# A late row is stored only where its token has its last late expert; GpSimd gathers the last eight tiles, then the last expert's sums

## The chip, the core and the metric

One core of one Trainium2 chip runs the kernel. The time is device microseconds of one launch. TensorE (PE) multiplies matrices, VectorE (DVE) and ScalarE (ACT) work on elements, GpSimd (POOL) does a few element operations and issues every transfer whose rows are found by an index, SyncE (SP) issues plain transfers; 16 DMA engines move the data.

## What is computed

One layer of a hybrid block over 2048 tokens of width 1024 in float32: a mixer (gated short convolution beside a gated delta rule), then a mixture of 32 experts in which each token goes to two, then a root-mean-square norm. What the change touches is the end:

```python
x = x + concat([y_a, y_b]) @ w_out              # after the mixer
h = rms_norm(x, ffn_norm_g)
# two experts e for every token, with a gate each:
y_e = (silu(h @ w_gate[e]) * (h @ w_up[e])) @ w_down[e]
x = x + sum(gate_e * y_e for the token's two experts)
return rms_norm(x, final_norm_g)
```

## The kernel before

The first 1150 us compute the mixer; the tokens' sums `x` then lie in DRAM as `acc_d`, the normed rows as `h2_d` (`h_d` in the profile), the gates as `gt_d`. While that ends, the router finds each token's experts (`OH`, `pos`) and, for every expert, a table of its tokens: `tabG` (rows to gather), `tabS` (rows to scatter to; an empty place has an index beyond the last row and is skipped) and `gix`. The experts are ranked by their number of tokens, and each rank has a fixed capacity of rows (`CAPS`); the last three ranks (`LAST = 3`, the "late" experts) have 120, 116 and 112 rows.

The loop over `jobs` runs the 32 experts. For each, SP loads the weights through staging tiles (`mst`) and ACT and DVE split them into float16 pairs (`wgu`, `wd`, L92 and L93); GpSimd gathers the expert's rows (`xr`, L1014) and gates (`gs`, L1019); PE turns them and multiplies (`gate_up`, L1045; `down`, L1080 or L1115); ACT scales the result into `yo`, and GpSimd adds it to the tokens' rows of `acc_d` by a scatter that accumulates (L1058). A scheduler orders each engine's instructions by the order of the code, woven by `weave`, and by `issue_after`, which puts an instruction behind another.

The final norm runs beside the last experts. The 2048 tokens are 16 tiles of 128. A token without a late expert is finished before the last three experts are, so its row can be normed early: `bix` holds a tile's row numbers, and for a token with a late expert an index beyond the last row. `load` (L1342) gathers a tile's rows of `acc_d` by `bix`: tiles 0 to 7 early into `mst`, tiles 8 to 15 late into `xw`. `norm_all` squares four tiles on ACT (`square`, L1330), makes one over the root on DVE and GpSimd (`root`, L1333 and the power at L1334), multiplies by it and by the gain on DVE (`gain`, L1337), and stores: tiles below `NPL` with a plain store by SP (L1374), the others by GpSimd with `bix` (L1378), so that rows of late tokens are left out.

The late tokens come last. `rows_of` (L1385) gathers for the last expert (rank 31, 112 rows) its tokens' rows of `acc_d` into `J.base`, here called the base; this can start only when the scatter of rank 30 has landed. DVE adds the last expert's result to it (L1087), and it is written back to `acc_d` without accumulating (L1406). The same gather fetches into `ends` the rows of ranks 29 and 30 (120 and 116 rows). All three are normed (`norm_rows`) and stored by `tabS` (`store_rows`, L1396). A token may have two late experts; then its row stands in two of the three sets, and only the later set has the whole sum. So these three stores write the same rows of `out` and are held in order: each waits until the one before has landed.

Around the change the order on GpSimd is: scatter of rank 30, base, two `ends`, eight late tiles (`load_late` puts them behind the last of the `rows_of`), the write of the base, the powers, four stores by `bix`, three by `tabS`. A GpSimd transfer uses one of eight semaphores in turn and waits until the transfer eight before it has landed.

## Time and profile before

| | us |
|---|---|
| median of 3 runs | 1951.93 (1949.07 to 1955.11) |
| the profiled execution | 1950.76 |
| its span | 1949.0 |
| PE busy | 1750.1 (90%) |
| DVE busy | 1402.3 (72%) |
| ACT busy | 1007.7 (52%) |
| POOL busy | 426.6 (22%) |

The span is the time from the first to the last instruction on the chip; the profiled execution took 1.76 us more around it. Busy shares are means over stages with different limits: the last PE instruction ends at 1880.3 us, so the last 69 us have no matrix work, and what lies there is read from the waits and the order of time in that stretch. The times in the sections below are microseconds from the start of the span.

### The profile page before, as it was taken

The numbers are of one execution on the slowest core, as the hardware profiler recorded it, in microseconds if no ns is written. First come the engines' busy times: TensorE is split into PE (matmuls) and PEld (weight loads), VectorE is DVE, ScalarE is ACT, GpSimd is POOL, SyncE is SP. The second block draws the span as 40 slices with busy tenths as digits, with TensorE's granted clock in tenths as the row PEclk, the third lists the DMA queues.
The fourth block names the chain that finished last, engine by engine and source line by source line (L and its number), as shares of the span: only waits on it lengthen the run. The fifth ranks groups of instructions, "written<-read, shape, count | busy, mean of one in ns | idle before, by whom it ended". The sixth has DMA issues, their size and how long they took to land.

```text
span 1949.0 us, 41805 instructions
## 1 busy us (share of the span) xinstructions
PE 1750.1 (90%) x16213; PEld 1198.9 (62%) x16213; DVE 1402.3 (72%) x2708; ACT 1007.7 (52%) x1674; POOL 426.6 (22%) x375
## 2 busy tenths in 40 slices
PE   7789999999999999999999959999989999999840
PEld 5455555555555554444454438788888899999730
DVE  8989888888888745322244768887778888888732
ACT  5655434444444324211234636766667777777621
POOL 1321111121111100000000012233222344344343
PEclk9989999999999999999999979999999999999975
DMA  4122001001001105002255967999999999999873
GB/s 143 67 64 56 11 15 44 18 11 47 20 11 37 36 19 165 28 15 57 98 175 197 342 231 236 347 306 311 309 315 349 360 332 345 349 343 316 286 233 136
DMA packets 203597, 330.27 MB, mean 169 GB/s; under 512 B 44590, under 2 KB 98935, under 8 KB 203394
## 3 DMA queue, kind: packets, MB, share of 16 engines
q1 hardware_dynamic: 178738, 271.20, 40.8%
q0 software_dynamic: 20128, 47.30, 9.5%
q10 hardware_dynamic: 4528, 9.06, 1.2%
q8 instruction: 129, 2.11, 0.4%
q14 instruction: 74, 0.61, 0.1%
HBM read 276.05 MB, written 54.82 MB: 170 GB/s over the span
## 4 chain that ended last, share of the span: by engine, by line
PE 31%; DMA 17%; DVE 9%; issue 5%; ACT 3%; SPq 1%; POOL 1%; DVEq 0%; ACTq 0%; POOLq 0%
PE acc L134 11%; PE a L1045 9%; DMA mst<-in_w_up_dram 9%; PE a L965 5%; DMA mst<-in_w_down_dram 4%; DVE wgu L93 2%; DMA mst<-in_w_gate_dram 2%; ACT wgu L92 1%; SPq L766 1%; PE pn L548 1%; DMA end<-acc_d,tabG 1%; PE pl L1102 1%; DVE yt L1121 1%; DVE xT L1031 1%; DVE wd L93 1%
## 5 line engine op out<-in xcount | busy, mean ns | idle before, releaser
L134 PE MATMUL acc<-hT,whl 128*128 128x512 f16 x2640 | 635.4, 381 | 0.2 <-DVE hT L203 0.2
L134 PEld LDWEIGHTS <-whl 128*128 128x128 f16 x2640 | 252.8, 99 | 248.4 <-issue 11.3
L1045 PE MATMUL a<-xT,wgu 128*128 128x128 f16 (+17 forms) x6144 | 394.8, 227 | 5.0 <-DVE sl L1052 2.2
L1045 PEld LDWEIGHTS <-wgu 128*128 128x128 f16 x6144 | 388.7, 99 | 12.0 <-issue 6.3
L93 DVE SCALAR_TENSOR_TENSOR wgu<-mst,gw,wgu 128x1024 f16<-128x1024 f32 x256 | 317.6, 1276 | 20.1 <-ACT wgu L92 19.6
L92 ACT ACTIVATE wgu<-mst,gw 128x1024 f16<-128x1024 f32 x256 | 280.2, 1139 | 34.8 <-DMA mst<-in_w_up_dram 32.7
L965 PE MATMUL a<-wo,yb 128*128 128x512 f16 x768 | 176.0, 381 | 0.0
L93 DVE SCALAR_TENSOR_TENSOR wd<-mst,wd 128x1024 f16<-128x1024 f32 x128 | 154.1, 1214 | 4.1 <-ACT wd L92 4.1
L1058 POOL DMA_INDIRECT acc_d<-yo,tabS x50 | 96.8, 1936 | 262.2 <-ACT yo L1106 190.2
L92 ACT ACTIVATE wd<-mst 128x1024 f16<-128x1024 f32 x128 | 131.2, 1047 | 21.4 <-DMA mst<-in_w_down_dram 21.4
L1115 PE MATMUL a<-ac,wd 128*128 128x144 f16 (+12 forms) x1824 | 136.3, 230 | 2.8 <-ACT ac L92 1.7
L1115 PEld LDWEIGHTS <-wd 128*128 128x128 f16 x1824 | 124.2, 98 | 5.4 <-issue 3.8
L965 PEld LDWEIGHTS <-yb 128*128 128x128 f16 x768 | 72.1, 98 | 79.4 <-issue 2.7
L294 DVE SCALAR_TENSOR_TENSOR cv<-raw,pcol,cv 128x512 f32<-128x512 f32 x144 | 118.1, 822 | 1.6
L1014 POOL DMA_INDIRECT xr<-h_d,tabG x51 | 59.9, 1174 | 173.0 <-PE t L1030 167.0
L1052 DVE SCALAR_TENSOR_TENSOR sl<-a,sl 128x128 f32<-128x128 f32 (+17 forms) x128 | 38.3, 300 | 81.3 <-ACT sl L1051 71.9
L1051 ACT ACTIVATE sl<-a 128x128 f32<-128x128 f32 (+17 forms) x128 | 35.9, 281 | 115.5 <-PE a L1045 109.9
L1080 PE MATMUL pl<-wd,ac 128*128 128x512 f16 (+4 forms) x312 | 77.4, 395 | 5.5 <-DVE ac L93 3.1
L382 DVE TENSOR_TENSOR pr<-Ts,fs 32x1 f32<-32x1 f32 (+14 forms) x240 | 76.7, 320 | 3.9 <-DMA fs<-dscr 0.3
L1019 POOL DMA_INDIRECT gs<-gt_d,gix x51 | 74.7, 1465 | 15.6 <-issue 15.6
L1102 PE MATMUL pl<-id,yt 128*128 128x128 f32 (+13 forms) x304 | 52.5, 291 | 24.7 <-ACT yo L1106 18.2
L545 ACT ACTIVATE osq<-acv 128x512 f32<-128x512 f32 x16 | 10.0, 628 | 124.7 <-DVE acv L543 124.7
(352 smaller groups left out, 2535.5 us busy)
## 6 DMA issues: line engine op xcount, KB each, us to landing
mst<-in_w_gate_dram SPq DMA_DIRECT2D x256, 256.0 KB
mst<-in_w_up_dram SPq DMA_DIRECT2D x256, 256.0 KB
mst<-in_w_down_dram SPq DMA_DIRECT2D x128, 512.0 KB
wst<-in_w_in_dram SPq DMA_DIRECT2D x28, 512.0 KB
xt<-in_x_dram SPq DMA_DIRECT2D x16, 512.0 KB
ydr<-yh SPq DMA_DIRECT2D x64, 128.0 KB
x<-in_x_dram SPq DMA_DIRECT2D x16, 512.0 KB
yb<-ydr SPq DMA_DIRECT2D x16, 512.0 KB
```

The lines of the kernel that those rows point to most:

```text
L92: A.activation(hi, src, AF.Copy, scale=scale)
L93: (eng or V).scalar_tensor_tensor(lo, src, scale, hi, op0=OP.mult, op1=OP.subtract)
L134: T.matmul(acc, w[:, i, k, :], hT[b][:, j, k, :], start=(n == 0), stop=(n == 3 * KT - 1))
L294: V.scalar_tensor_tensor(y, tap(j), pcol[:, q:q + 1], y, op0=OP.mult, op1=OP.add)
L382: V.tensor_tensor(q, Ts[:, 0:i, 0:i].rearrange("p j m -> p m j"), bc(fs[:, None, 0:i, i], [32, i, i]), op=OP.mult)
L965: T.matmul(po, yb[:, i, k, c * P:(c + 1) * P], wo[:, j, k, n * FF:(n + 1) * FF], start=(q == 0), stop=(q == 3 * KT - 1))
L1019: G.indirect_dma_start(out=g[0:cw], out_offset=None, in_=gt_d[0:end * NE, :], in_offset=IO(ap=gx, axis=0))
L1045: T.matmul(pg[:, q, 0:n], wq[:, i, k, q, f * P:(f + 1) * P], xT[:, j, k, 0:n], start=(z == 0), stop=(z == 3 * KT - 1))
L1058: st = G.indirect_dma_start(out=acc_d, out_offset=IO(ap=sx, axis=0), in_=yo[0:cw], in_offset=None, bounds_check=S - 1, oob_is_err=False, c ...
L1080: T.matmul(py[0:n], ac[:, i, k, 0:n], wd[:, j, k, q * FF:(q + 1) * FF], start=(z == 0), stop=(z == 3 * FF // P - 1))
L1102: T.transpose(py[0:cw, c * P:(c + 1) * P], yts[d2][:, u, off:off + cw], id32)
L1115: T.matmul(pg[:, u, 0:n], wd[:, i, k, d * P:(d + 1) * P], ac[:, j, k, 0:n], start=(z == 0), stop=(z == 3 * FF // P - 1))
```

## The change

Four edits:

1. `others` also finds each token's last late rank: `cc16` now holds 1, 2, 3 for ranks 29, 30, 31 and 0 for the others (it was 1 or 0), and the larger of the token's two values is kept, 64 more where the token does not fit into the expert's capacity. It goes with the token's number into a DRAM table `fl_d` (one number per token). `visits` gathers that number for the rows of each of the three late ranks and makes `tabL` from it: the row number where this rank is the token's last late one, else an index beyond the last row.
2. The three late stores go by `tabL` instead of `tabS`. No row is then written twice, so they no longer wait for each other, and they stand before the last four tiles' stores.
3. `load_late` stands behind the scatter of rank 30 and not behind the `rows_of`; the base and the two `ends` stand behind the last of the late tiles.
4. `NPL` falls from 12 to 8: tiles 8 to 11 are stored by GpSimd with `bix` and not by SP. Tiles 8 to 11 are normed ahead of the late rows.

```diff
-        V.tensor_scalar(cc16[:, 1:2], rc[:, 1:2], float(NE - LAST), None, op0=OP.is_ge)
+        V.tensor_scalar(cc16[:, 1:2], rc[:, 1:2], float(LAST - NE + 1), 0.0, op0=OP.add, op1=OP.max)
...
     def others():
...
+        V.tensor_tensor(m[:, 1], pos, m[:, 1], op=OP.is_ge)
+        V.scalar_tensor_tensor(m[:, 0], m[:, 1], FAR, m[:, 0], op0=OP.mult, op1=OP.add)
+        yield 1
+        V.tensor_tensor(m[:, 2, 1], m[:, 0, 0], m[:, 0, 1], op=OP.max)
+        V.scalar_tensor_tensor(fl[:, :, 0], m[:, 2, 1], BIG, tok, op0=OP.mult, op1=OP.add)
+        nc.gpsimd.dma_start(fl_d.rearrange("(t p) c -> p t c", p=P), fl)
...
+    def visits():
+
+        for l in range(LAST):
+            G.indirect_dma_start(out=flp[:, l:l + 1], out_offset=None, in_=fl_d,
+                                 in_offset=IO(ap=tabG[:, NE - LAST + l, 0:1], axis=0))
+            yield 1
+        to = tabS[:, NE - LAST:, 0]
+        V.tensor_tensor(flp, flp, lrow, op=OP.subtract)
+        V.scalar_tensor_tensor(tabL, flp, 2.0 * S, to, op0=OP.add, op1=OP.max)
...
-    NPL = NT - GT
+    NPL = AHEAD
...
-        with tc.issue_after(gathers[0]):
+        with tc.issue_after(adds[-1].ins):
             for t in range(AHEAD, NT):
...
-                    st = G.indirect_dma_start(out=out2, out_offset=IO(ap=bix[:, t:t + 1], axis=0), in_=xs[t],
-                                              in_offset=None, bounds_check=S - 1, oob_is_err=False)
-                    apart(st, outs + stores)
-                    stores.append(st)
+                    store_rows(xs[t], bix[:, t:t + 1], plain)
...
-            J.base = [rows_of(J.chunks[0][0], J.n, stage())]
-            ends = [(rows_of(L.chunks[0][0], L.n, o1.tile([P, D], F32, name="end", tag="hh")), L.chunks[0][2])
-                    for L in jobs[-LAST:-1]]
             load_late()
+            with tc.issue_after(loads[-1].ins):
+                J.base = [rows_of(J.chunks[0][0], J.n, stage())]
+                ends = [rows_of(L.chunks[0][0], L.n, o1.tile([P, D], F32, name="end", tag="hh")) for L in jobs[-LAST:-1]]
...
+        elif left == 1:
+            parts.append((behind(slices(na, 2 * GT), marks[-1]), 2 * GT, 0, 0.5))
...
     def rest():
-        for x, sx in ends:
+        for x in ends:
             norm_rows(x)
-        yield from slices(na, 2 * GT)
-        norm_rows(J.base[0][0:J.n], end)
-        yield from slices(na, 2 * GT)
-        for x, sx in ends + [(end, J.chunks[0][2])]:
-            store_rows(x, sx)
+        norm_rows(J.base[0][0:J.n], end)
+        for i, x in enumerate(ends + [end]):
+            store_rows(x, tabL[0:x.shape[0], i:i + 1])
+        yield from slices(na, 2 * GT)
```

What it moves on the engines, as the order of their instructions shows it. On GpSimd, from the scatter of rank 30 (L1058) to the last store, before; `mst` with `tabG` is the base, `xw` a late tile, and the words in brackets are the semaphores that a row waits for (DMASW: GpSimd's own transfers, DMAHW: SP's):

```order
L1058 DMA acc_d<-yo,tabS 2048x1024 [waits DMASW6_49,DMASW3_49,Activation_49]
L1334 TENSOR_TENSOR ss_24193<-ss_24193,mhalf 128x4 [waits DVE_49]
L1385 DMA mst<-acc_d,tabG 112x1024 [waits DMAHW6_49,DMASW4_49,DMASW3_49]
L1385 DMA end<-acc_d,tabG 120x1024 [waits DMASW5_49,PE_49]
L1385 DMA end<-acc_d,tabG 116x1024 [waits PE_49]
L1342 DMA xw<-acc_d,bix 128x1024 [waits DMASW7_49,PE_49]
...
L1378 DMA out_dram<-xw,bix 2048x1024 [waits DMASW3_49,DVE_49]
L1396 DMA out_dram<-end,tabS 2048x1024 [waits DMASW4_49]
L1396 DMA out_dram<-end,tabS 2048x1024 [waits DMASW5_49,DMASW4_49]
L1396 DMA out_dram<-mst,tabS 2048x1024 [waits DMASW6_49,DMASW5_49]
```

And now, the same stretch:

```order
L1059 DMA acc_d<-yo,tabS 2048x1024 [waits DMASW7_49,DMASW2_49,Activation_49]
L1371 DMA xw<-acc_d,bix 128x1024 [waits DMASW0_49,PE_49]
...
L1371 DMA xw<-acc_d,bix 128x1024 [waits DMASW7_49]
L1412 DMA mst<-acc_d,tabG 112x1024 [waits DMAHW6_49,DMASW0_49]
L1412 DMA end<-acc_d,tabG 120x1024 [waits DMASW1_49]
L1412 DMA end<-acc_d,tabG 116x1024 [waits DMASW2_49]
L1363 TENSOR_TENSOR ss_24211<-ss_24211,mhalf 128x4 [waits DVE_49]
...
L1423 DMA out_dram<-end,tabL 2048x1024 [waits DVE_49]
L1423 DMA out_dram<-mst,tabL 2048x1024 [waits DVE_49]
L1423 DMA out_dram<-xw,bix 2048x1024 [waits DMASW3_49,DVE_49]
```

The eight `xw` gathers have moved ahead of the base, the last of them waits for semaphore 7 (that of the scatter), the power for tiles 4 to 7 (`ss_24193`, now `ss_24211`) has moved from ahead of the gathers to behind them, and the late stores no longer wait for each other.

On DVE, from the last expert's multiplications on, before; `ss_24193` belongs to tiles 4 to 7, `ss_24459` and `ss_24484` to tiles 8 to 11 and 12 to 15:

```order
L1337 SCALAR_TENSOR_TENSOR mst<-mst,ss_24193,gfin 128x1024 [waits DMASW7_49,Pool_49]
...
L1087 SCALAR_TENSOR_TENSOR mst<-pl,gs,mst 112x512 [waits DMASW6_49,DMASW4_49,PE_49]
...
L1337 SCALAR_TENSOR_TENSOR end<-end,ss_24447,gfin 120x1024 [waits DMASW5_49,Pool_49]
L1337 SCALAR_TENSOR_TENSOR end<-end,ss_24453,gfin 116x1024 [waits DMASW6_49,Pool_49]
L1337 SCALAR_TENSOR_TENSOR xw<-xw,ss_24459,gfin 128x1024 [waits DMASW7_49,Pool_49]
...
L1337 SCALAR_TENSOR_TENSOR mst<-mst,ss_24478,gfin 112x1024 [waits Pool_49]
L1333 TENSOR_SCALAR ss_24484<-ss_24484 128x4 [waits Activation_49]
L1337 SCALAR_TENSOR_TENSOR xw<-xw,ss_24484,gfin 128x1024 [waits DMASW3_49,Pool_49]
```

And now:

```order
L1362 TENSOR_SCALAR ss_24433<-ss_24433 128x4 [waits Activation_49]
L1088 SCALAR_TENSOR_TENSOR mst<-pl,gs,mst 112x512 [waits DMASW2_49,DMASW0_49,PE_49]
...
L1366 SCALAR_TENSOR_TENSOR mst<-mst,ss_24211,gfin 128x1024 [waits DMASW3_49,Pool_49]
...
L1366 SCALAR_TENSOR_TENSOR xw<-xw,ss_24433,gfin 128x1024 [waits Pool_49]
...
L1366 SCALAR_TENSOR_TENSOR end<-end,ss_24492,gfin 120x1024 [waits DMASW1_49,Pool_49]
L1366 SCALAR_TENSOR_TENSOR end<-end,ss_24498,gfin 116x1024 [waits DMASW2_49,Pool_49]
L1366 SCALAR_TENSOR_TENSOR mst<-mst,ss_24504,gfin 112x1024 [waits Pool_49]
L1366 SCALAR_TENSOR_TENSOR xw<-xw,ss_24519,gfin 128x1024 [waits DMASW4_49,Pool_49]
```

The four gains of tiles 4 to 7 have moved behind the base's sum (L1087, now L1088), and those of tiles 8 to 11 ahead of the three late ones.

At the start of the experts, on DVE in the first expert's `gate_up` (`sl` is the gated product, `ac` its float16 pair), the two rows that make `tabL` are new:

```order
L1053 SCALAR_TENSOR_TENSOR sl<-a,sl 128x128 [waits Activation_49]
L93 SCALAR_TENSOR_TENSOR ac<-sl,ac 128x128 [waits Activation_49]
L1246 TENSOR_TENSOR flp<-flp,lrow 128x3 [waits DMASW7_49,DMASW6_49,DMASW0_49]
L1247 SCALAR_TENSOR_TENSOR tabL<-flp,tabS 128x3 [waits DVE_49]
L1053 SCALAR_TENSOR_TENSOR sl<-a,sl 128x128 [waits Activation_49]
L93 SCALAR_TENSOR_TENSOR ac<-sl,ac 128x128 [waits Activation_49]
L1053 SCALAR_TENSOR_TENSOR sl<-a,sl 128x128 [waits Activation_49]
```

They stand between the second and the third of the first expert's four parts and wait for three GpSimd transfers. Ahead of them DVE has a second product and sum over `OH` (128x1024 each) and a few rows of 16 or 32 columns more, and GpSimd the store of `fl_d` and the three gathers.

## Rows read from the trace of the kernel before

**Rows 1.** PE's last matrix work: start, us, engine, line, what.

```profile
1874.79 5.48 PE L1080 MATMUL pl<-wd,ac 128*112 128x512 f16 x24
```

**Rows 2.** Waits from 1860 us on: who for what, us in total, times, longest.

```profile
ACT jk L1330 <- DMA end<-acc_d,tabG: 21.3, 2, 14.0
...
POOL out_dram L1396 <- DMA out_dram<-end,tabS: 12.2, 2, 8.5
DVE mst L1087 <- DMA mst<-acc_d,tabG: 11.0, 1, 11.0
POOL mst L1385 <- DMA acc_d<-yo,tabS: 10.7, 1, 10.7
```

**Rows 3.** GpSimd in order of time: start, us, what, idle before it and its releaser.

```profile
1866.72 2.17 POOL L1058 DMA_INDIRECT acc_d<-yo,tabS  x1 [7.88 <-ACT yo L1089]
1868.09 1.89 POOL L1334 TENSOR_TENSOR ss<-ss,mhalf 128x4 f32<-128x4 f32 x1
1880.65 1.02 POOL L1385 DMA_INDIRECT mst<-acc_d,tabG  x1 [10.67 <-DMA acc_d<-yo,tabS]
...
1884.86 1.04 POOL L1342 DMA_INDIRECT xw<-acc_d,bix  x1 [0.30 <-issue]
...
1900.75 0.99 POOL L1406 DMA_INDIRECT acc_d<-mst,tabS  x1 [0.30 <-DVE ss L1333]
1901.75 1.12 POOL L1334 TENSOR_TENSOR ss<-ss,mhalf 120x1 f32<-120x1 f32 x2
...
1916.99 1.83 POOL L1378 DMA_INDIRECT out_dram<-xw,bix  x1 [1.61 <-DVE xw L1337]
1919.13 2.01 POOL L1378 DMA_INDIRECT out_dram<-xw,bix  x1 [0.31 <-DVE xw L1337]
...
1928.73 1.27 POOL L1396 DMA_INDIRECT out_dram<-end,tabS  x1 [3.68 <-DMA out_dram<-end,tabS]
1938.48 0.95 POOL L1396 DMA_INDIRECT out_dram<-mst,tabS  x1 [8.48 <-DMA out_dram<-end,tabS]
```

**Rows 4.** DVE in order of time, the same columns.

```profile
1870.01 1.28 DVE L1337 SCALAR_TENSOR_TENSOR mst<-mst,ss,gfin 128x1024 f32<-128x1024 f32 x1 [1.43 <-POOL ss L1334]
...
1888.12 1.41 DVE L1087 SCALAR_TENSOR_TENSOR mst<-pl,gs,mst 112x512 f32<-112x512 f32 x2 [11.04 <-DMA mst<-acc_d,tabG]
...
1905.68 2.48 DVE L1337 SCALAR_TENSOR_TENSOR end<-end,ss,gfin 120x1024 f32<-120x1024 f32 x2
...
1915.41 4.87 DVE L1337 SCALAR_TENSOR_TENSOR xw<-xw,ss,gfin 128x1024 f32<-128x1024 f32 x4 [1.20 <-POOL ss L1334]
```

**Rows 5.** GpSimd's DMA queue, 1869 to 1880 us: packets, MB, share of 16 engines.

```profile
q0 software_dynamic: 479, 0.42, 22.8%
```

**Rows 6.** The same, 1880 to 1909 us.

```profile
q0 software_dynamic: 2033, 5.45, 58.8%
```

**Rows 7.** The same, 1928 to 1939 us.

```profile
q0 software_dynamic: 484, 0.42, 14.0%
```

**Rows 8.** All DMA, 1939 to 1949 us in 40 slices, tenths busy.

```profile
DMA  0000999774100000000000000000000000000000
```

**Rows 9.** DVE where the new table is made, in order of time.

```profile
1163.48 1.21 DVE L1211 TENSOR_TENSOR pq<-OH,rank 128x1024 f32<-128x1024 f16 x1
...
1170.52 0.17 DVE L1218 TENSOR_TENSOR bix<-om,tok 128x16 int32<-128x16 f32 x1
...
1181.21 0.29 DVE L1052 SCALAR_TENSOR_TENSOR sl<-a,sl 128x128 f32<-128x128 f32 x1 [1.62 <-ACT sl L1051]
```

**Rows 10.** GpSimd there.

```profile
1155.36 0.79 POOL L906 DMA_DIRECT2D gt_d<-gt  x1 [12.31 <-DVE Ms L870]
...
1172.18 0.98 POOL L1019 DMA_INDIRECT gs<-gt_d,gix  x1 [0.30 <-issue]
```

**Rows 11.** Engines' busy time, granted clock, DMA share, GB/s there.

```profile
1180.00:1185.00 5.00, 5.00 (x71) 4.10 (x69) 1.99 (x5) 2.45 (x6) 0.98 (x1) 1.00 0.00 0
```

**Rows 12.** GpSimd beside a busy DVE, in order of time.

```profile
1842.68 6.60 POOL L1342 DMA_INDIRECT mst<-acc_d,bix  x1 [0.31 <-DVE wgu L93]
```

More of the change, by code (lines that the diff above doesn't have):

```diff
@@ L732, in hybrid_block @@
     gt_d = dram.tile([S * NE, 1], F32, name="gt_d")
+    fl_d = dram.tile([S, 1], F32, name="fl_d")
     rt = ctx.enter_context(tc.tile_pool(name="rt", bufs=1, reuse_waits="tile"))
@@ L1319, in hybrid_block @@
     GT = 4
-    NPL = NT - GT
-    loads, stores, adds, outs, gathers = [], [], [], [], []
+    NPL = AHEAD
+    loads, adds, outs, plain = [], [], [], []
     def apart(st, others):
@@ L1376, in norm_all @@
                         tc.add_manual_dep(st.ins, adds[-1].ins.name, SYNC, reason="the scatter goes first")
+                    plain.append(st)
                 else:
-                    st = G.indirect_dma_start(out=out2, out_offset=IO(ap=bix[:, t:t + 1], axis=0), in_=xs[t],
-                                              in_offset=None, bounds_check=S - 1, oob_is_err=False)
-                    apart(st, outs + stores)
-                    stores.append(st)
+                    store_rows(xs[t], bix[:, t:t + 1], plain)
                 yield 1
     def rows_of(ix, cw, xf):
-        gathers[:] = [G.indirect_dma_start(out=xf[0:cw], out_offset=None, in_=acc_d, in_offset=IO(ap=ix, axis=0)).ins]
+        G.indirect_dma_start(out=xf[0:cw], out_offset=None, in_=acc_d, in_offset=IO(ap=ix, axis=0))
         return xf[0:cw]
@@ L1393, in norm_rows, with store_rows @@
         gain(x, s, n, dst)
-    def store_rows(x, sx, more=True):
-        st = G.indirect_dma_start(out=out2, out_offset=IO(ap=sx, axis=0), in_=x, in_offset=None,
+    def store_rows(x, ix, others=()):
+        st = G.indirect_dma_start(out=out2, out_offset=IO(ap=ix, axis=0), in_=x, in_offset=None,
                                   bounds_check=S - 1, oob_is_err=False)
-        if more:
-            apart(st, stores)
+        if others is not None:
+            apart(st, outs + list(others))
             outs.append(st)
@@ L1476, in hybrid_block @@
         if j == 4:
-            parts.append((seq(ovf, others()), 11, 0, 1))
+            parts.append((seq(ovf, others()), 16, 0, 1))
+        elif j == 5:
+            parts.append((visits(), LAST + 1, 0.2, 1))
         if left == LAST:
@@ L1532, in hybrid_block @@
         norm_rows(x)
-        store_rows(x, ox[:, 0:1], False)
+        store_rows(x, ox[:, 0:1], None)
 _INS = ['x', 'mix_norm_g', 'w_in', 'conv_a_w', 'conv_a_norm_g', 'dn_conv_w', 'dn_a_log', 'dn_dt_bias', 'dn_norm_g',
```

25 lines of the change are left out of this document (17 added, 8 removed).

## The prediction

> **What bounds the kernel now.** I looked first for the end of the matrix work: PE stops at 1880.3 us (1874.79 and 5.48) of a span of 1949.0 [rows 1], so 69 us are a tail of transfers and norms. Second, the waits from 1860 us on [rows 2]. Four matter. GpSimd stands 10.7 us until the scatter of rank 30 has landed; DVE stands 11.0 us for the base; ACT stands 21.3 us for the two `ends`, 14.0 of them for the second; GpSimd stands 12.2 us between the three late stores. Third, GpSimd and DVE in order of time [rows 3, 4], read as one chain: scatter issued until 1868.9, base gathered from 1880.65, DVE multiplies without a pause that matters from 1905.7 to 1920.3, GpSimd's last store begins at 1938.5. DVE is thus done 19.2 us before the last store is out (1939.43): that part is stores that wait for each other. Fourth, the DMA queues, by the share of the 16 engines. While the scatter lands GpSimd's queue is busy for 22.8% [rows 5], so GpSimd waits beside engines that are mostly free; while the eleven gathers and the write of the base run it is 58.8% beside SP's stores [rows 6]. The two 116-row transfers are the slow ones: the scatter moves 0.42 MB in 11 us [rows 5], and the store of rank 30 has about three engines' worth of work (14.0% of 16 over 11 us is 24.6 engine-us, over the 8.2 us until its landing) [rows 3, 7]. The 112-row store is through in 1.75 us on nearly all engines [rows 8].
>
> **The late gathers moved ahead.** Up to the scatter's issue at 1866.7 the tail's instructions stand where they stood. Then eight gathers follow at 1.04 + 0.30 us each [rows 3] instead of a 10.7 us wait: seven go out from 1869.2 to 1878.5. The eighth uses the scatter's semaphore and so waits for its landing like the base did (1880.65); the base follows at 1882 and the `ends` until 1885.8, two transfers' issue later than the base before or less. So the gathers cost no GpSimd time that was in use. When the base lands is the open question. From the end of its issue it took 6.45 us (1881.67 to 1888.12) [rows 3, 4], beside four plain stores that are now later; the same would give 1889.4. The other bound: if the scatter holds about four engines until 1880 (22.8% of 16), the seven gathers' parts on those lie behind it. One gather is 5.45 / 12 = 0.45 MB; the queue moved 5.45 MB in 0.588 x 16 x 29 = 273 engine-us [rows 6], 0.020 MB per engine-us, so a gather is 1.4 us of each engine. Nine of them (seven, the eighth, the base) after 1880 end at 1892.8. I take 1891, between, a little nearer the row that shows the slow scatter; bounds 1887 (the plain stores gone) and 1892.8.
>
> [...] No run here has gathers behind a 116-row scatter.
>
> **The power of tiles 4 to 7.** It ran at 1868.1 [rows 3], ahead of the gathers, and its four gains on DVE from 1870.0, beside PE [rows 4]. Now it stands behind the `ends` and the gains behind the base's sum. That uncovers 4.87 us of DVE work (four gains as in [rows 4]) on a chain that DVE sets. In return the squares of tiles 8 to 11 are done while the base is awaited.
>
> **The sum of the tail.** Base 1891.0. DVE then: sum 1.41, tiles 4 to 7 4.87, tiles 8 to 11 4.87 [rows 4]: 1902.2. Behind that on GpSimd stand the write of the base (it waits for both `ends`, some 6 to 8 us after the base) and four stores, then the powers. A store beside a busy DVE took 1.83 and 2.01 us, else about 1.0 [rows 3], with 0.3 between. The five end at 1903.5 at the earliest (1.3 after the last gain) and at 1909.5 if all five are slow from 1898; I take 1905.5. This is the new wait: DVE's late gains need the powers that stand behind these stores. First power 0.56 (half of 1.12) [rows 3]: 1906.1. DVE: three late sets 3 x 1.24, last four tiles 4.87 [rows 4]: 1914.7. GpSimd's seven last stores end at 1916.0 if each follows its gain, at 1924.3 if all are slow from 1908.2; I take 1918. They no longer wait for each other; that is where the 12.2 us go.
>
> Landing: before, 1939.43 to about 1941.8 [rows 3, 8], 2.4 us, which gives 1920.4. But rank 30's store is now the second of seven, issued until about 1912. It held some engines for 8.5 us (end of its issue at 1930.0 to 1938.5) [rows 3], until 1920.5, and five stores of 1.4 us per engine queue behind it: 1927.6. I take 1925.5, nearer the latter, since that row is the same transfer. From the last packet to the end of the span is 7.2 us [rows 8]: 1932.7. The execution has 1.76 us around the span (1950.76 against 1949.0): 1934.5.
>
> **The four plain stores gone from SP.** SP has nothing behind them; tiles 8 to 11 cost GpSimd four issues, counted above. What is late next if DVE were faster: GpSimd's store issue.
>
> **The new table.** Added on DVE, next to the product of 1.21 us [rows 9]: another one, a sum that I take as equal, and about eight small rows at 0.17 [rows 9]: 3.8 us, beside PE's first `gate_up`; DVE is busy 1.99 of the 5 us from 1180 to 1185 [rows 11], so they fit, and `fl` and `bix` come at 1174.3 instead of 1170.5. Then on GpSimd: store of `fl_d` 0.8 (as for `gt_d`), three gathers at 0.98 + 0.30 [rows 10], and two landings, of which no row shows the time. Lower bound of a landing 1 us or so, upper the slowest of the trace: 11.6 for the scatter (1868.9 to 1880.5) and 14.0 for the `end`. With 2 us each the table is there at 1174.3 + 0.2 + 0.8 + 2 + 3.8 + 2 = 1183.1. DVE waits for it in front of the third `sl`, due at 1181.2 [rows 9]. Queued behind are the first expert's last two products, a copy and the splits of the next weights; the DMA engines are idle there (0.00) [rows 11] until the splits free staging tiles, so what is lost there is lost for the whole weight stream. Most of these 1.9 us lies before the fourth `sl` is due; I count 0.5 us, bounds 0 and 23.5 (both landings slowest). GpSimd's next gather, behind them, waits for PE and has its turn no later than before. The four added GpSimd transfers shift the turn of the semaphores by four; each still waits for the transfer eight before, so I count nothing.
>
> In all 1934.5 + 0.5 = **1935.0 us**, 15.8 below the profiled execution. The median of the runs lies 1.2 above that execution; I leave the forecast there, since that is inside the spread of the runs.
>
> **Rivals.**
> 1. GpSimd becomes the bound. Beside a busy DVE one gather took 6.60 us instead of 1.0 [rows 12]. If GpSimd gets nothing out while DVE multiplies, the five transfers start at 1902.2 (1908.7), the late gains end at 1917.9, and the seven stores at 1927; with 5 us to land, 7.2 and 1.76, and 0.5 for the table: 1941.5. For it: 1.83 and 2.01 beside four gains. Against: those two did go out. 15%.
> 2. Nothing queues. The base lands at 1888, stores run at 1.3, the last landing takes 2.4: 1888 + 11.15 + 1.3 + 0.6 + 8.6 + 1.3 + 2.4 + 7.2 + 1.8 + 0.5 = 1923. For it: the free engines [rows 5] and the 112-row store [rows 8]. 13%.
> 3. The gathers slow the scatter down. It is a chain of small steps at a quarter of the engines; with 3 MB beside it, it may take twice its 11 us, and base and `ends` wait for it. The sum shifts by 9 or so: 1944. 10%.
> 4. Slower than before: the wait of DVE for `tabL` in the first expert. Mechanism and place as above; price up to 23.5 us if `fl_d` and the gathers land as slowly as the slowest rows, carried to the end since the weight stream restarts behind it: 1934.5 + 23.5 = 1958. It decides from 16 us, that is if the table lands after 1197. Against: `fl_d` is 8 KB. 5%.
>
> That the change doesn't do what it says (late stores still in order) is excluded by the order of the instructions: they have no wait for each other.
>
> **How the numbers follow.** The forecast has 57%; rivals 1 to 4 as given. The range, 1923 to 1947, takes in rivals 1 to 3 and the bounds of the sum, and leaves out rival 4 and the far ends. A difference under 0.3% (5.9 us) is about what a measurement of this kernel can't tell from no change. Faster by more: the forecast, rivals 1 and 2, a little of 3, in all 86%. Within 0.3%: the rest of 3 and half-way cases of 4, 9%. Slower: 5%.
>
> **What the changed profile would show.** Right: seven `xw` gathers between 1869 and 1880; the base landing near 1891; no GpSimd wait for a late store's landing; DVE's last gain near 1915 and GpSimd's last issue near 1918. Wrong: the base after 1895 (rival 3), GpSimd stores of 2 us or more back to back (rival 1), a DVE wait of over 5 us in front of the third `sl` (rival 4), or an end of the matrix work later than 1880 by more than 1 us.

## The result, and the profile after

The changed kernel takes 1957.4 us (median; 1945.3 to 1965.9), the kernel before beside it 1946.7 (1941.9 to 1955.1). The ratio is 1.0052, with a 95% interval of 1.0040 to 1.0064: slower by half a per cent, where 1935 was forecast. The profiled execution after is 1954.53 us long with a span of 1952.8; before it was 1950.76 with 1949.0.

First the early part. GpSimd and then DVE, where the new table is made (start, us, engine, line, what, idle before it and its releaser):

```profile
1174.55 1.24 POOL L1233 DMA_DIRECT2D fl_d<-fl  x1
1184.50 0.99 POOL L1242 DMA_INDIRECT flp<-fl_d,tabG  x1 [8.71 <-DMA fl_d<-fl]
...
1187.05 0.94 POOL L1242 DMA_INDIRECT flp<-fl_d,tabG  x1 [0.30 <-issue]
```

```profile
1189.47 0.16 DVE L1246 TENSOR_TENSOR flp<-flp,lrow 128x3 f32<-128x3 f32 x1 [11.24 <-DMA flp<-fl_d,tabG]
...
1189.74 0.28 DVE L1053 SCALAR_TENSOR_TENSOR sl<-a,sl 128x128 f32<-128x128 f32 x1
```

The engines over two stretches of 5 us there (busy us of PE, PEld, DVE, ACT, POOL, then granted clock, DMA share, GB/s), to be held against [rows 11]:

```profile
1180.00:1185.00 5.00, 3.41 (x44) 2.44 (x41) 0.00 (x0) 0.00 (x0) 0.50 (x1) 1.00 0.01 3
1185.00:1190.00 5.00, 0.00 (x0) 0.00 (x0) 0.50 (x3) 0.00 (x0) 3.37 (x4) 0.85 0.03 3
```

The 8 KB of `fl_d` land 8.7 us behind their issue. Three gathers follow, and DVE stands 11.2 us in front of the third `sl`, which comes at 1189.7 instead of 1181.2 [rows 9]. For 5 us PE and ACT have nothing, and hardly any DMA runs (0.03). That delay is still there when the matrix work ends:

```profile
1871.65 10.32 PE L1046 MATMUL a<-xT,wgu 128*128 128x112 f16 x178
1881.81 5.35 PE L1081 MATMUL pl<-wd,ac 128*112 128x512 f16 x24
```

PE ends at 1887.2, 6.9 us later than in [rows 1]. Now the tail, GpSimd in order of time (against [rows 3]):

```profile
1873.89 2.17 POOL L1059 DMA_INDIRECT acc_d<-yo,tabS  x1 [8.09 <-ACT yo L1090]
1876.37 1.08 POOL L1371 DMA_INDIRECT xw<-acc_d,bix  x1 [0.31 <-issue]
...
1887.87 0.98 POOL L1371 DMA_INDIRECT xw<-acc_d,bix  x1 [2.62 <-DMA acc_d<-yo,tabS]
1889.16 0.95 POOL L1412 DMA_INDIRECT mst<-acc_d,tabG  x1 [0.30 <-DMA xw<-acc_d,bix]
...
1903.90 9.02 POOL L1433 DMA_INDIRECT acc_d<-mst,tabS  x1 [8.85 <-DVE mst L1366]
1913.22 1.01 POOL L1423 DMA_INDIRECT out_dram<-xw,bix  x1 [0.31 <-issue]
...
1918.08 3.98 POOL L1363 TENSOR_TENSOR ss<-ss,mhalf 120x1 f32<-120x1 f32 x4
1922.29 5.84 POOL L1423 DMA_INDIRECT out_dram<-end,tabL  x1 [0.22 <-issue]
...
1935.09 0.96 POOL L1423 DMA_INDIRECT out_dram<-xw,bix  x1 [0.30 <-issue]
```

and DVE (against [rows 4]):

```profile
1901.06 1.41 DVE L1088 SCALAR_TENSOR_TENSOR mst<-pl,gs,mst 112x512 f32<-112x512 f32 x2 [7.37 <-DMA mst<-acc_d,tabG]
1902.38 4.86 DVE L1366 SCALAR_TENSOR_TENSOR mst<-mst,ss,gfin 128x1024 f32<-128x1024 f32 x4
1907.16 4.86 DVE L1366 SCALAR_TENSOR_TENSOR xw<-xw,ss,gfin 128x1024 f32<-128x1024 f32 x4
...
1918.71 2.48 DVE L1366 SCALAR_TENSOR_TENSOR end<-end,ss,gfin 120x1024 f32<-120x1024 f32 x2 [6.42 <-POOL ss L1363]
...
1922.31 4.87 DVE L1366 SCALAR_TENSOR_TENSOR xw<-xw,ss,gfin 128x1024 f32<-128x1024 f32 x4
```

The write of the base into `acc_d` lasts 9.02 us on GpSimd (0.99 in [rows 3]), from 1903.9 until just after DVE's eight gains end (1912.0). The first late store lasts 5.84, until just after the next gains end (1927.2). DVE in turn stands 6.42 us for a power that is queued behind that write and four stores. The store waits of [rows 2] are gone, as intended: from the scatter's issue to the end of the span it is 78.9 us, against 82.3 before.

### The profile page after: what moved, and what is told of

It reads as the page before. It is cut to its first block, busy times and chain, and to the rows that moved or that the text cites. A ratio compares the mean times of both kernels' runs of the same rounds, so it can differ in the third digit from the quotient of the medians.

```text
span 1952.8 us, 41824 instructions
## 1 busy us (share of the span) xinstructions
PE 1751.2 (90%) x16213; PEld 1199.2 (61%) x16213; DVE 1404.7 (72%) x2715; ACT 1009.4 (52%) x1674; POOL 445.7 (23%) x384
## 5 line engine op out<-in xcount | busy, mean ns | idle before, releaser
L92 ACT ACTIVATE wgu<-mst,gw 128x1024 f16<-128x1024 f32 x256 | 280.6, 1139 | 31.9 <-DMA mst<-in_w_up_dram 31.8
L92 ACT ACTIVATE ac<-sl 128x128 f16<-128x128 f32 (+17 forms) x128 | 40.3, 315 | 63.9 <-DVE sl L1053 63.9
```

Source lines behind the costliest of these rows:

```text
L92: A.activation(hi, src, AF.Copy, scale=scale)
```

## The stages of all kernels

Three numbers from each trace, which the experiments are read by. **Front**: from the first silu row on ACT to DVE's first weight split (before: 1175.93 to 1184.49). **Stream**: from the first expert's scatter to the last. **Tail**: from that last scatter's issue to the end of the span. The ratio is to the kernel before on the same chip, with its 95% interval.

| kernel | front | stream | tail | ratio |
|---|---|---|---|---|
| before (two traces) | 8.6, 8.6 | 676.5, 675.4 | 82.3, 81.8 | |
| changed (two traces) | 17.0, 17.4 | 675.7, 678.6 | 78.9, 79.5 | 1.0052 (1.0040 to 1.0064) |
| a1_wait_later | 9.8 | 680.6 | 79.5 | 1.0006 (0.9991 to 1.0021) |
| a2_table_only | 15.7 | 682.8 | 84.2 | 1.0066 (1.0047 to 1.0084) |
| a3_flat64 | 9.1 | 679.8 | 77.7 | 0.9986 (0.9976 to 0.9996) |
| a4_late_psum | 13.5 | 676.3 | 67.8 | 0.9947 (0.9933 to 0.9961) |
| b1_write_last | 17.1 | 679.3 | 78.9 | 1.0055 (1.0039 to 1.0072) |
| b2_all | 8.6 | 680.3 | 67.8 | 0.9982 (0.9969 to 0.9995) |
| b3_early_pow | 8.6 | 685.3 | 70.0 | 0.9970 (0.9957 to 0.9984) |
| c4_no_write_move | 8.6 | 686.5 | 66.6 | 0.9973 (0.9959 to 0.9987) |
| d4_order | 17.4 | 681.5 | 84.5 | 1.0070 (1.0053 to 1.0086) |
| e1_mended | 9.6 | 680.9 | 67.2 | 0.9941 (0.9928 to 0.9955) |
| *rank 30 with 120 rows:* | | | | |
| c1_before120 | 8.6 | 671.2 | 66.6 | 0.9903 (0.9887 to 0.9919) |
| c2_after120 | 15.4 | 670.9 | 74.0 | 0.9984 (0.9970 to 0.9998) |
| c3_later_psum_120 | 9.5 | 669.2 | 64.4 | 0.9897 (0.9881 to 0.9913) |
| b4_cap120 | 8.6 | 674.9 | 57.7 | 0.9896 (0.9878 to 0.9914) |
| d1_order_120 | 8.6 | 677.8 | 62.2 | 0.9913 (0.9898 to 0.9928) |
| e2_mended_120 | 9.5 | 675.6 | 61.8 | 0.9891 (0.9876 to 0.9905) |

## The early wait

Three kernels: the wait moved, the table alone, and the store of `fl_d` in larger pieces.

a1_wait_later:
```
-            parts.append((visits(), LAST + 1, 0.2, 1))
+            parts.append((behind(visits(), latest()), LAST + 1, 0.2, 1))
```


> The changed kernel with one thing moved: the two DVE rows that turn the three gathered columns into the store table (L1246, L1247) stand about one expert later on DVE; the fl_d store and its three gathers on GpSimd stay where they are. Theory (the early wait is one half of the loss): DVE no longer stands 11.2 us before the first expert's slot row, the first weight split is back from 1191.6 us to 1184 to 1185.5, the scatter of the last expert but one from 1873.9 to 1866.5 to 1868, PE's end from 1887.2 to about 1880.5, and the time is 6 to 7.5 us below the changed kernel. Rival (the early delay is in the added DVE and GpSimd work itself, eight rows and three gathers, not in the wait): the scatter stays within 2 us of 1873.9 and the time within 2 us of the changed kernel. The tail behind the scatter should stay as it was, 78 to 80 us, by both.

a2_table_only, in the kernel before:
```
-            parts.append((seq(ovf, others()), 11, 0, 1))
+            parts.append((seq(ovf, others()), 16, 0, 1))
+        elif j == 5:
+            parts.append((visits(), LAST + 1, 0.2, 1))
```
(with the changed kernel's `others`, `visits` and `fl_d`)

> The kernel before with the new table alone: the added rows on DVE, the fl_d store and its gathers, at the places that they have in the changed kernel; the stores at the end go as before and the table is read by nobody. Theory (early wait): the scatter of the last expert but one is issued 6.5 to 7.5 us later than before (1866.72), and the time is 6 to 8 us above the kernel before. Rival (the later start is absorbed on the way, the late scatter of the changed kernel comes from the new tail): the scatter stays within 1.5 us of 1866.7, the time within 2 us of the kernel before.

a3_flat64:
```
-        nc.gpsimd.dma_start(fl_d.rearrange("(t p) c -> p t c", p=P), fl)
+        nc.gpsimd.dma_start(fl_d.rearrange("(p t) c -> p t c", p=P), fl)
...
-                                 in_offset=IO(ap=tabG[:, NE - LAST + l, 0:1], axis=0))
+                                 in_offset=IO(ap=flx[:, l:l + 1], axis=0))
```


> The changed kernel with fl_d laid out so that a partition stores its sixteen numbers as one piece of 64 bytes instead of sixteen pieces of 4 bytes; the gathers take a changed index, four more small DVE rows ahead of them. Theory (the fl_d store lands 8.7 us after its issue since its 2048 pieces are small): the landing falls to 2 to 3.5 us behind the issue, DVE's wait of 11.2 us falls to 4 to 6, and the time is 4 to 6.5 us below the changed kernel. Rival (the landing is slow for another reason, the queue or the completion path): it stays at 8 to 9 us, and the time within 1.5 us of the changed kernel.

GpSimd and DVE of a3_flat64, the rows that answer to those of the changed kernel:

```profile
1173.16 0.60 POOL L1235 DMA_DIRECT2D fl_d<-fl  x1
1175.86 0.97 POOL L1248 DMA_INDIRECT flp<-fl_d,flx  x1 [2.10 <-DMA fl_d<-fl]
```

```profile
1181.04 0.16 DVE L1252 TENSOR_TENSOR flp<-flp,lrow 128x3 f32<-128x3 f32 x1 [3.09 <-DMA flp<-fl_d,flx]
```

The same 8 KB in 128 pieces of 64 bytes land in 2.10 us instead of 8.71 in 2048 pieces of 4, and DVE waits 3.09 us. That alone takes the ratio from 1.0052 to 0.9986, about 13 us; moving DVE's wait instead takes about 9 (1.0006), and the table put into the kernel before costs 13 (1.0066, between 9 and 16). So the table's wait costs 9 to 13 us by three ways of asking, as much as the whole loss or more, and the layout of the store in small pieces is its cause (the number of pieces, their size and their spacing changed together and weren't told apart). In a1_wait_later GpSimd itself still stood 8.99 us for `fl_d`, with the next rows of activations queued behind; the front was 9.8 there, but 13.5 in the trace of a4_late_psum, which has the same early part.

The signs came as the theories had them, the sizes did not. All three expected 4 to 8 us; a1 gave 9, a2 and a3 about 13, of which the front explains 7.1 and 7.9. In a2 the last scatter is 12.0 us late (1878.67), since the stream is 6.3 us longer too, and no row shows why. The absolute times in a1's expectation (scatter back at 1867) were missed, since the first silu row came 2.5 us later than before in that execution and the stream was 4 us longer; by the scatter of this one trace (1874.58) its rival would stand, and only the front and the timed ratio speak against it. Hence the stages above, and the ratios.

## GpSimd beside DVE's gains

a4_late_psum, on top of a1:
```
+        if left == 1:
+            ...
+                gps += [psA.tile([P, FF], F32, name="a") for _ in range(2)]
+                for q in range(2):
+                    A.activation(gps[q], gfin[:, q * FF:(q + 1) * FF], AF.Copy)
...
-        V.scalar_tensor_tensor(x if dst is None else dst, x, s, gfin[0:n], op0=OP.mult, op1=OP.mult)
+            for q in range(2):
+                c = slice(q * FF, (q + 1) * FF)
+                V.scalar_tensor_tensor(dst[:, c], x[:, c], s, gps[q][0:n], op0=OP.mult, op1=OP.mult)
```


> a1_wait_later, and besides it the gain vector is copied to PSUM (two tiles of 512 columns) during the last expert, so that the gains of the last eight tiles and of the late rows, two half rows each, read one input from SBUF and one from PSUM. Theory (GpSimd's issue is held up by DVE's rows with two inputs in SBUF): the write of the last expert's sums into acc_d falls from 9.02 us to 1 to 2.5, the first late store from 5.84 to 1 to 2.5, the pows from 2.0 and 4.0 for their groups to 1.3 and 2.5 at most, and the time is 8 to 12 us below a1_wait_later (less 0.5 to 2 us if a half row from PSUM takes longer). Rival (the write is long because the DMA queue or its rings hold it, whatever DVE does): 9.0 and 5.8 us stay within 1 us and the time stays within 2 us of a1_wait_later.

DVE and GpSimd of a4_late_psum; the gains with `gfin` still read two inputs in SBUF, those with `a` read one in PSUM:

```profile
1900.97 4.86 DVE L1374 SCALAR_TENSOR_TENSOR mst<-mst,ss,gfin 128x1024 f32<-128x1024 f32 x4
1905.75 5.35 DVE L1372 SCALAR_TENSOR_TENSOR xw<-xw,ss,a 128x512 f32<-128x512 f32 x8
...
1916.94 5.35 DVE L1372 SCALAR_TENSOR_TENSOR xw<-xw,ss,a 128x512 f32<-128x512 f32 x8
```

```profile
1903.03 3.69 POOL L1441 DMA_INDIRECT acc_d<-mst,tabS  x1 [9.10 <-DVE mst L1374]
1907.43 1.01 POOL L1431 DMA_INDIRECT out_dram<-xw,bix  x1 [0.71 <-DVE xw L1372]
...
1912.35 2.62 POOL L1363 TENSOR_TENSOR ss<-ss,mhalf 120x1 f32<-120x1 f32 x4
1915.19 1.07 POOL L1431 DMA_INDIRECT out_dram<-end,tabL  x1 [0.22 <-issue]
```

The write is held only while the gains with `gfin` run (until 1905.8) and is out 0.9 us later; beside the gains from PSUM the four stores take 1.0 us each, and the late store 1.07 instead of 5.84. The gains are 10% longer (5.35 against 4.86), and the tail is still 11.7 us shorter than a1's; the times differ by as much (1.0006 and 0.9947, 11.5 us). This is the other failed step, shown by taking the cause away. One thing was not separated: the edit also cuts each gain into two rows of half the length. That a row's end alone doesn't free GpSimd is argued from the changed kernel, where the write was held past the ends of six gains. The kernel before with its gains from PSUM was not run; there two stores were held by about 1 us each [rows 3]. The traces show beside what an indirect DMA's issue is long, 9.02 us beside `scalar_tensor_tensor` rows with two inputs in SBUF and 0.97 to 1.07 beside those with one; by what it is held no run here shows.

b1_write_last:
```
-        if J.base:
-            ...
-            st = G.indirect_dma_start(out=acc_d, out_offset=IO(ap=sx, axis=0), in_=J.base[0][0:cw], in_offset=None,
...
         yield from slices(na, 2 * GT)
+        with tc.issue_after(outs[-1].ins):
+            write_base(J)
```


> The changed kernel with one row moved: the write of the last expert's sums into acc_d (L1433), which took 9.02 us of GpSimd beside DVE's gains and is read by the overflow loop alone, stands behind the last store of out_dram. Theory (any DMA row of GpSimd is held up while DVE runs its gains with two inputs in SBUF): the first store of a late tile takes the write's place, lasts 4 to 6 us from about 34.5 us behind the scatter's issue (after its tile's gain) to 39 us, when DVE's eight gains end (38.1), and the time is 0.5 to 2 us below the changed kernel. Rival (the write is slow by itself: its rows go to the tensor that the gathers ahead of it read): the first store lasts 1 to 2 us, the four stores end 4 to 5 us sooner, and the time is 4 to 6 us below the changed kernel.

GpSimd of b1_write_last:

```profile
1914.70 4.21 POOL L1423 DMA_INDIRECT out_dram<-xw,bix  x1 [13.88 <-DVE xw L1366]
...
1926.98 5.83 POOL L1423 DMA_INDIRECT out_dram<-end,tabL  x1 [0.22 <-issue]
```

With the write out of the way the first store is the one that is held, 4.21 us, until just after DVE's gains end (1918.0); tail 78.9, time as the changed kernel's (0.5 to 2 us less was expected). It isn't the write, it is whatever GpSimd has there. How long a row is held varies: two stores beside four such gains took 1.83 and 2.01 in [rows 3]. What lets a row slip in between two gains wasn't found.

## Both repairs together

b2_all is a1, a3, a4 and b1 in one; b3_early_pow moves the pow of tiles 4 to 7 ahead of the gathers; c4_no_write_move is b2 without b1.

> The changed kernel with four repairs together: fl_d in pieces of 64 bytes (a3_flat64), the two table rows of DVE an expert later (a1_wait_later), the late gains from PSUM (a4_late_psum), the write of the last expert's sums behind the stores (b1_write_last). By the theory (early wait and held-up GpSimd, which add): the front as in a3_flat64, first weight split 8.5 to 9.2 us behind the first silu row, the tail 65 to 67.5 us from the scatter's issue to the end of the span (a4_late_psum: 67.8), 16 to 21 us below the kernel before by the two stages' rows and, with the stream's own spread between executions, a ratio of 0.990 to 0.993. Rival (a3_flat64 gained where a4_late_psum did already, so the two don't add): the ratio stays at 0.994 to 0.996.

b3_early_pow:
```
             root(s)
+            if t0 == GT:
+                late_loads()
...
-                        tc.add_manual_dep(st.ins, adds[-1].ins.name, SYNC, reason="the scatter goes first")
+                        tc.add_manual_dep(st.ins, loads[-1].ins.name, SYNC, reason="the last tiles go first")
```


> b2_all, and the pow of tiles 4 to 7 stands ahead of the eight gathers of late tiles on GpSimd, so that DVE gains those tiles beside PE's last expert and not behind the last sums; their plain stores wait for the last of the eight gathers. Theory (behind the sums the end is a chain of DVE gains and GpSimd stores, 4.86 us of it for tiles 4 to 7): the tail is 3 to 5 us shorter than that of b2_all, the ratio 0.0015 to 0.0025 below it. Rival (the gathers start a pow later, and the plain stores share the DMA engines with the gathers of the last rows, so that the sums come in later by as much): tail and time within 1.5 us of b2_all.

c4_no_write_move, in b2:
```
-        with tc.issue_after(outs[-1].ins):
-            write_base(J)
```


> b2_all without its fourth repair: the write of the last sums stands ahead of the stores again, as in the changed kernel; 116 rows. b2_all came out at 0.9982 of the kernel before, a4_late_psum, without this and without the 64-byte pieces, at 0.9947. Theory (the spread of the expert stream between executions and chips, not the write, made the difference; the two tails were 67.8 us both): within 0.0015 of b2_all, 0.9965 to 0.9997. Rival (the write as the last transfer of all costs the end its landing): 0.991 to 0.995.

b2_all and b3_early_pow missed; c4_no_write_move came within its theory's band, so the place of the write isn't what separates b2 from a4. All three are at 0.997 to 0.998, 4 to 7 us slower than a4_late_psum relative to before, with the front as it should be, and in b2 and c4 the tail (b2's is 0.3 us above its band). In b3 the base's sum comes 31.9 us behind the scatter's issue instead of 26.6 in b2, so that what the early pow gains is lost there, as its rival had it; the time is within noise of b2's. All three streams are longer than a4's, and the trace shows one wait that a4 doesn't have. DVE of b2_all:

```profile
1292.71 0.16 DVE L1252 TENSOR_TENSOR flp<-flp,lrow 128x3 f32<-128x3 f32 x1 [8.19 <-DMA flp<-fl_d,flx]
```

The new index rows sat inside `visits`, so when a1's edit held `visits` back it now held the gathers back too, and DVE waited 8 to 9 us for them about an expert later. Here the kernel had a fault that the theory didn't know of: it moved the wait where a1 had removed it. The mended edit puts the index rows into `others` and holds back only the last two rows.

e1_mended (the changed kernel with a3, a1 and a4 done so):
```
-            parts.append((visits(), LAST + 1, 0.2, 1))
+            parts += [(visits(), LAST, 0, 0.2), (behind(table(), latest()), 1, 0.2, 1)]
```


> The changed kernel (116 rows) with the index rows of the 64-byte layout at the place of the table, the three gathers of fl_d early, DVE's two table rows an expert later, and the late gains from PSUM; the write of the last sums as in the changed kernel. Theory (the two failed steps are all that separates the change from its forecast): DVE waits for no gather of fl_d, neither early nor at 1290 us, the first weight split stands 8.5 to 9.5 us behind the first silu row, the stream from the first scatter to the last is 675 to 679 us (d3_before_again: 675.4), the tail 66 to 68 us, and the time is 0.9915 to 0.994 of the kernel before, 12 to 16 us. Rival (something else in the changed kernel lengthens the stream): stream 680 us or more, ratio 0.995 to 0.999 as b2_all and c4_no_write_move.

No wait for `flp` is left in its trace, front 9.6, tail 67.2: 0.9941, 11.5 us faster than before, a hair above the band expected. By the timed runs that is 8 us better than b2_all, clear of both intervals. The stream of its trace, though, is 680.9, as the rival said, and b2's is 680.3 with the wait; so the traces don't show that the wait made the stream longer. And a4_late_psum, with the small pieces left as they were, is at 0.9947: once DVE's wait is moved, larger pieces give nothing more that can be measured.

## What the new place of the gathers is worth

d4_order, one part of the change undone:
```
-            load_late()
-            with tc.issue_after(loads[-1].ins):
-                J.base = [rows_of(J.chunks[0][0], J.n, stage())]
-                ...
+            J.base = [rows_of(J.chunks[0][0], J.n, stage())]
+            ...
+            load_late()
```


> The changed kernel with one part of the change undone: the gathers of the last expert's rows and the end rows stand ahead of the eight gathers of late tiles again (116 rows, the early wait and the gains in SBUF as in the changed kernel). It keeps the new stores, without waits among them. Theory (the waits among the late stores, 12.2 us, were the change's real gain, and the gathers' new place brings little, since the sums then come in behind eight tiles): the tail is 66 to 72 us instead of 78.9, the early stage stays at 17 us, the ratio 0.996 to 1.0005, that is 8 to 16 us below the changed kernel. Rival (the gathers' new place is worth what the prediction gave it): the tail is 80 us or more, the ratio 1.005 or more.

The theory fell: the tail is 84.5 us, longer than the changed kernel's by 5 to 6 (the ratios, 1.0070 and 1.0052, overlap in their intervals). Waits of d4_order from 1860 us on (who for what, us in total, times, longest):

```profile
ACT jk L1359 <- DMA xw<-acc_d,bix: 24.0, 1, 24.0
```

The squares of the late tiles, first on ACT, then wait 24 us for tiles gathered last. a2_table_only, with the same gathers' order and the same table but the stores of before, has a tail of 84.2 and a ratio of 1.0066: without the gathers' new place the free stores gain nothing. That the new place is a gain of 5 to 6 us stands on the tails of the traces alone. All this holds with GpSimd held up beside the gains; with 116 rows and the gains from PSUM the old order wasn't run.

## The rows of rank 30

b4_cap120, in b2:
```
-             132, 132, 128, 128, 124, 124, 124, 120, 120, 120, 116, 112]
+             132, 132, 128, 128, 124, 124, 124, 120, 120, 120, 120, 112]
```


> b2_all with the last expert but one given 120 rows instead of 116. [...] Rival (the queue is bound by its total bytes, and the end rows aren't waited for): the time within 1.5 us of b2_all, on the upper side by the 0.4 us that PE pays for four columns more (4 of 116 of an expert's matmuls).

c1_before120 and c2_after120 are the same edit in the two kernels. The narrow transfers are those of 116 rows: in the kernel before rank 30's scatter keeps 22.8% of the 16 engines busy [rows 5] and its store 20.5% (1931 to 1937 us), where the store of rank 29's 120 rows keeps 74.6% busy (1926 to 1927.5 us).

> The kernel before with 120 rows instead of 116 for the last expert but one, nothing else. [...] Rival (b4_cap120's gain needs the new tail, whose gathers stand in another order): less than 8 us below it.

> The changed kernel with 120 rows instead of 116 for the last expert but one, nothing else; against c1_before120 it gives the price of the change where the narrow transfers are gone. Theory (the change pays 8 to 9 us for the table's early wait and up to 12 us for GpSimd's issue beside DVE, and what it takes away, the waits behind narrow transfers, is mostly gone at 120 rows): 6 to 14 us above c1_before120. Rival (the order of the stores was the gain, and it is independent of the rows): within 3 us of c1_before120 or below it.

b4_cap120 gained 17 us on b2_all by the ratios (0.9896 against 0.9982), far more than the 2 to 4 us that its author had forecast, and c1 lies in the 12 to 25 us forecast for it; both rivals fell. Four more rows, in the kernel before and nothing else: 0.9903, 19.7 us faster by the medians. GpSimd of c1_before120, against [rows 3]:

```profile
1867.84 0.98 POOL L1385 DMA_INDIRECT mst<-acc_d,tabG  x1 [4.85 <-DMA acc_d<-yo,tabS]
...
1917.89 0.95 POOL L1396 DMA_INDIRECT out_dram<-mst,tabS  x1 [3.29 <-DMA out_dram<-end,tabS]
```

GpSimd's DMA queue while that scatter lands, 1863 to 1868 us (against [rows 5]):

```profile
q0 software_dynamic: 144, 0.41, 55.5%
```

The waits of 10.67 and 8.48 are 4.85 and 3.29, the scatter uses 55.5% of the engines for 5 us instead of 22.8% for 11, and the tail falls from 82.3 to 66.6. In the mean that is 3.6 engines of 16 for the 116 rows and 8.9 for the 120. Why four rows more keep more engines busy no run here shows.

With 120 rows the change as it was given costs 16 us (0.9984 against 0.9903; 6 to 14 were expected): 6.9 of front and 7.4 of tail by the traces. c2 shows a third cost. PE's last expert there:

```profile
1883.10 0.41 PE L1046 MATMUL a<-xT,wgu 128*128 128x112 f16 x5 [1.10 <-issue]
1884.56 0.36 PE L1046 MATMUL a<-xT,wgu 128*128 128x112 f16 x4 [1.05 <-issue]
...
1893.15 1.19 PE L1046 MATMUL a<-xT,wgu 128*128 128x112 f16 x11 [1.15 <-issue]
```

Matmuls in bursts of one to six, up to 1.15 us apart, with nothing that the profile names to wait for. While they last the granted clock falls: it is 1.00 until 1885 us, after two us in which PE was busy for 0.41 and 0.36 us, and 0.50 from there to 1898, and the last 24 matmuls take 7.58 us instead of 5.35. PE ends 26 us behind the scatter's issue instead of 13.3 (changed kernel), and the base's sum waits for it. Such gaps are in eight of fourteen traces with the gathers ahead of the scatter's landing (a1, a3, a4, c2, c3, c4, e1, e2) and in none of the six without. With 116 rows the base lands later than PE ends anyway: in the changed kernel its sum begins 27.2 us behind the scatter's issue, and in e1_mended, with gaps, 27.3, where PE ends after 20.7. With 120 the gaps count: the base's sum begins 19.5 us behind the scatter's issue in b4_cap120 without them, 25.6 and 25.2 in c3 and e2 with them, and the tails are 57.7, 64.4 and 61.8 (c3 and e2 also have the write ahead of the stores, b4 doesn't).

> a4_late_psum with 120 rows: the table's rows on DVE later, the late gains from PSUM, the wider last expert but one; fl_d in 4-byte pieces and the write of the last sums ahead of the stores, as in the changed kernel. Against b4_cap120 (0.9896 of the kernel before) it tells whether those two are worth anything once the rest is mended. Theory (the store of fl_d still holds GpSimd 8.5 to 9 us early, and the next expert's rows stand behind it): 2 to 6 us above b4_cap120, a ratio of 0.990 to 0.993. Rival (they are worth nothing, as a4_late_psum against b2_all suggests): 0.986 to 0.990.

> e1_mended with 120 rows for the last expert but one. Theory: against b4_cap120 (0.9896) it loses the wait of 8.9 us at 1290 us, of which 2 to 7 us had come through to the end: 0.986 to 0.988, if PE's last expert runs without gaps; with them the tail is 63 to 66 us and the ratio up to 0.990. Rival (the wait at 1290 us is made up for later in the stream): 0.9885 or more without gaps.

d1_order_120 has b4's repairs and the gathers in the order of before:

> b4_cap120 with the gathers of the last rows ahead of the eight gathers of late tiles again, as in the kernel before. Theory (the early gathers take the DMA engines from PE's last expert in some executions, and with 120 rows the scatter lands 5 us behind its issue, so that there is little to win by going ahead of it): PE's last matmuls run without gaps, PE ends 13 to 15 us behind the scatter's issue, the tail is 55 to 60 us (b4_cap120: 57.7, c3_later_psum_120 with gaps: 64.4, c1_before120: 66.6) and the time is 0.984 to 0.988 of the kernel before. Rival (late tiles that come in last are the longer wait): the tail is 62 us or more and the ratio 0.989 or more.

No gaps, but late tiles come later: tail 62.2, ratio 0.9913, the rival's. c3 came out as its rival had it, and e2 in its band for a trace with gaps, with a tail 1.2 us below it. c3, b4, d1 and e2 all lie within 0.9891 and 0.9913, and so does c1: once rank 30 has 120 rows, the change with its two faults mended is worth nothing that can be measured against the kernel before with the same rows. These are the fastest versions seen.

The two further traces:

> The changed kernel, unchanged, one more trace. Where the trace in hand is typical: first weight split 17.0 us behind the first silu row (within 0.5), the stream from the first scatter to the last 674 to 680 us, PE's last expert without gaps, tail 78.9 (within 1.5). Where PE's gaps come by execution and not by kernel, they may show here, with PE's end 18 to 25 us behind the scatter's issue instead of 13.3.

> The kernel before, unchanged, one more trace. Where the trace in hand is typical: first weight split 8.6 us behind the first silu row, the stream from the first scatter to the last 676.5 us (within 1.5), tail 82.3 (within 1). Where it was a short one, and the kernels with the table are no longer in their stream: 679 to 684 us.

Both are as the first ones, front and tail within 0.6 us; the changed kernel has no gaps in either. What stays open: in twelve traces of kernels with 116 rows and the table the stream is 675.7 to 686.5, in the two of before 676.5 and 675.4. Three of them (b2, b3, c4) have the wait at 1290 us, but e1 without it is no shorter than b2, and e2 (675.6) no shorter than b4 with it (674.9); for the others no row shows why either. And the changed kernel lies some 4 us further above the one before than front and tail add up to (10 by the ratio, against 8.5 to 8.8 of front less 2.3 to 3.4 of tail).

## Why the prediction was wrong

Its times are set against the trace less 7.17 us, the delay of the scatter (1873.89 against 1866.72).

- **The table: failed, the landing was mis-sized.** "With 2 us each" took a landing for which no row stood, as did its lower bound of 1 us; both were the author's estimate. `fl_d` took 8.7. DVE's wait was 11.2 us instead of 1.9, and the 0.5 us counted became 7.2 in this execution. Rival 4 named the mechanism, with its place and a price up to 23.5 us, but gave it 5% and put the point from which it decides at 16 us, on the strength of 8 KB being little. The number of pieces was in the code: 2048.
- **The gathers: right, the base's landing mis-sized.** The eighth goes out at 1880.7 (forecast 1880.65), the base at 1882.0 (1882). The scatter isn't slowed at all (13.98 us from its issue to that of the eighth gather, which waits for it; 13.93 to the base's before), so rival 3 fell. The base is used at 1893.9, 2.9 later than taken and 1.1 beyond the upper bound, the one by which the gathers queue behind the scatter's parts. That they queue there was the author's estimate; the trace shows the landing alone, 10.95 us from the end of the base's issue (1890.11) to its use, against 6.45 before.
- **The power and the gains: right.** From base to the end of eight gains 10.96 us (11.15); from the first late gain to the last 8.5 (8.6).
- **GpSimd's stores: failed.** The write and four stores end at 1910.9, beyond the bound of 1909.5; the last store at 1928.9, not 1918, beyond 1924.3. The slow end took 2.01 us a row from [rows 3] and set aside the 6.60 of [rows 12] as rival 1 (15%); measured were 9.02 and 5.84. Rival 1's mechanism is what happened: GpSimd got almost nothing out while DVE multiplied.
- **The landing: near.** The last store is issued at 1936.05; all DMA from 1936 to 1953 us in 40 slices, as in [rows 8]:

```profile
DMA  9999997544211111000000000000000000000000
```

The last packets go in the sixteenth slice, by 1942.8: 6.8 us (7.5 taken, by an estimate of what queues behind rank 30's store, which no run here shows). From there to the end it is 10 instead of 7.2, for which no row here shows why.

In sum for this execution: 6.7 us of delay at the scatter (7.17 less 0.5) and 12.9 of tail make up the 19.5 by which 1954.53 misses 1935.0. Of the 12.9 the base's landing is 2.9, the two groups of stores 2.7 and 5.6, and the end behind the last packet 2.8; the other terms are less than 1 us off and take back the rest. With both faults mended the tail is 67.2 against 66.0 forecast (1932.7 less 1866.7), and the time 0.9941 of before, 11.5 us faster where 15.8 was forecast. That the two tails agree so well is in part luck: the base's sum begins 27.3 us behind the scatter's issue in e1_mended, where 24.3 was forecast, and a gain from PSUM is 10% longer. The idea was worth most of what it was priced at; the two things that it brought along cost as much and more.

## What to carry to other kernels

A small table that goes through DRAM costs its landing, which here fell from 8.7 to 2.1 us with 128 pieces in place of 2048: lay it out so that a partition stores one piece, and put the row that waits for it behind work that doesn't. Before moving GpSimd's DMA issues beside a chain of DVE rows with two SBUF inputs, move one of those inputs to PSUM, or count the issue as lasting, at worst, to the end of the chain, as it did here with 9.02 and 5.84 us (about 1 us beside gains from PSUM). And look at the row counts first: 120 rows instead of 116 in one expert were worth more here, 19.7 us in the kernel before, than the whole reordering, 11.5 us with its faults mended.

## What was not expected of the hardware

- A store of 8 KB in 4-byte pieces: 8.5 to 9.0 us to land (8.71 in the changed kernel, 8.99 in a1_wait_later, 8.49 in a4_late_psum); in 64-byte pieces 2.1 to 2.2 (2.10 in a3_flat64, 2.19 in e1_mended).
- An indirect DMA's issue on GpSimd beside DVE gains from SBUF: 3.5 to 10.2 us in most kernels with the change (9.02 and 5.84 in the changed kernel, 10.15 in c2_after120), but 1.7 to 2.1 for two stores each in the kernel before, a2, c1 and d4; beside gains from PSUM 1.0 to 1.3 (1.07 and 1.26 for the first two late stores of a4_late_psum).
- A scatter of 116 rows: waited for 10.7 us in the kernel before; of 120 rows, 4.85 in c1_before120.
- PE's matmuls with gaps of 0.2 to 1.15 us while gathers run, in some traces, and in c2_after120 the granted clock at 0.50 behind them; the cause of the gaps wasn't tested.
